# Mixture-of-experts layer: the sum of the experts' rows into the tokens in steps of eight products instead of four

## Chip, cores and metric

One core of a Trainium2 chip runs the whole layer as one program. The time is the device time of one execution in microseconds (us). Three runs of the kernel before gave 1341.96, 1343.40 and 1344.57 us: the median is 1343.4. A trace of one more execution gives what each engine did: TensorE (PE, its weight loads apart as PEld), VectorE (DVE), ScalarE (ACT), GpSimd (POOL) and SyncE (SP), which issues the weight DMAs.

## What is computed

A decoder layer for 512 tokens of width 1024: a mixer (a convolution group and a dilated-attention group), a LayerNorm, a mixture of 32 experts of which each token takes 4, and a second LayerNorm. The change lies in the part with the experts:

```
logits = xt @ router_w + router_b
top_logit, top_idx = top_k(logits, 4);  gate = softmax(top_logit)
# per expert e, for the tokens that chose it:
g = min(xb @ w_gate[e] + b_gate[e], 7);  u = clip(xb @ w_up[e] + b_up[e], -7, 7)
y = ((u + 1) * g * sigmoid(1.702 * g)) @ w_down[e] + b_down[e]
out[token] += gate * y                    # the sum of the change
x = layer_norm(alpha * x + out)
```

All of it is in float32. Each expert has three 1024x1024 matrices, 12 MB, which are read from memory once: some 400 MB in all.

## The kernel before

The mixer and the first LayerNorm take the first 270 us and are the same in both kernels. Behind them comes the main pass over the experts.

**Rows and groups.** A *row* is a set of 32 token slots of one expert. The table `TURNS` gives the order of the experts and how many rows each has: expert 0 has three, then 2, 2, 3, 3, 2, 3, 4, 2, 2, 3, 2, 4, 2, 2, 3, 2, 4, 2, 4, 2, 2, 3, 4, 2, 2, 3, 4, 3, 2, 1, 1 for experts 1 to 31. Here "expert n" is the place in this order. Four rows in a line make a *group* of 128 slots (22 groups). The tokens of a group are gathered with indirect DMAs on POOL, one for each row (L1017). Rows of one expert may lie in one group or in two.

**One expert** (`expert`, L1066) goes through six pieces of weights of 2 MB. Pieces 0 to 3 are gate and up: for each row 8 matmuls into the row's own PSUM bank (L1078; an f32 matmul stands in the trace as two records, so 16 records for a row and piece). After piece 3, each row goes through `swiglu` on DVE and ACT (L1059 to L1064), which ends with the transposed hidden values `hT`. Pieces 4 and 5 are the down product: two rows of one group together (L1104, 512 columns) or one row (L1107, 256 columns). It can start when `hT` of its rows is there. At the end ACT and DVE write the result as an upper part `yh` and a lower part `yl` (L1121, L1123).

**The sum** (`combine`, L1125) adds a group's rows to the 512 tokens in `acc`: a one-hot matrix `cg` from DVE (L1129), then for each of four tiles of 128 tokens and each half of the columns two products, `cg` with `yh` and `cg` with `yl`, into one PSUM bank of the pool `cb` (L1135, L1136), and one add on DVE (L1137). That is 16 products and 8 adds for a group. The pool `cb` has three banks; `gd` has four for the experts' own results and `sl` has one.

**What sets the order.** Each engine takes its instructions in the order in which they are written. `combine` is a generator: it stops at each `yield`, and `fill` goes on with it up to the next one. After each of an expert's six pieces `tick` calls `fill` once (`FILLS` is six ones), so that one step stands behind each piece. What stands between piece 3 and piece 4 stands on PE between the last gate and up product and the first down product, which waits for `hT`. A group's sum is put in line (L1494 in the kernel before) when the next expert uses no row of it any more. Before the last expert's end `ENDC` lets all that is left run in one go.

Of the kernel before, what the change touches and what calls it, by code (L numbers as in the profile page):

```python
# [27 lines left out]
# Experts are taken in an order of falling token count (expert 0 first, whatever its count); the  # L28
# place in that order sets how many blocks of 32 token slots an expert gets in the main pass.
# Tokens beyond an expert's slots are taken by the loop behind it, 128 at a time.  # L30
# [3 lines left out]
# the blocks of the places, in the order of the main pass: light and heavy ones take turns, as the loads set the pace  # L34
# [3 lines left out]
def plan():  # L38
    """Places in the order that the main pass takes them, each with its rows (group, row)."""
    by = {n: [p for p in range(1, NE) if NBLK[p] == n] for n in (4, 3, 2, 1)}  # L40
    seq = [0] + [by[int(n)].pop(0) for n in TURNS[1:]]
    rows, n = [], 0
    for p in seq:
        if p == seq[-1]:
            n = -(-n // 4) * 4
        rows.append((p, [((n + b) // 4, (n + b) % 4) for b in range(NBLK[p])]))
        n = max(n + NBLK[p], 4)
    return rows, -(-n // 4)


# column ranges of the constant array
# [28 lines left out]
# how many working buffers the mixer has  # L80
# [10 lines left out]
# how many of a channel's taps the tensor engine makes, and GpSimd adds up  # L91
# [23 lines left out]
class Buf:  # L115
    """Space of one kind: taken when the first task that uses it is placed, given back after the last."""
# [5 lines left out]
class Plan:  # L122
    """The order of a long stretch of instructions: tasks with an engine, a rough duration (us) and what they
    read and write are placed one by one where they can start first; of several, the one with the longest
    path behind it (less its group's lag) goes first. Spaces of a kind are given out in program order; of a bank,
    one engine has to be done before another can begin."""
# [58 lines left out]
    def order(self, lags):  # L185
        """[(start, end, task, engine, {space: place})]"""
# [78 lines left out]
def tile_layer(ctx: ExitStack, tc: tile.TileContext, x, positions, w_in, conv_w, conv_b, conv_ln_g,  # L265
# [22 lines left out]
    def piece():  # L288
        """The next place of the ring, when there is room."""
        i = turn.pop(0)  # L290
        turn.append(i)
        count[0] += 1
        return ring[i].rearrange("p (k a) f -> p k (a f)", a=2)

    def expert_loads(tag, e):
        """The six loads of one expert's weights."""
# [22 lines left out]
    def advance(used=1):  # L319
        """Pieces have been used up: start the loads that now have room."""  # L320
        freed[0] += used
        while stream and count[0] - freed[0] < size[0]:
            stream.pop(0)()
# [24 lines left out]
    # ================= mixer =================  # L348
# [24 lines left out]
    def warm(t, n):  # L373
        """Products that nobody reads: the tensor engine's clock is halved after a pause."""
        for _ in range(n):
            P.matmul(t.rearrange("p (a c) -> p a c", a=4), onesb, onesb[:, None, :].to_broadcast([128, 4, 128]), start=True,
                     stop=True)

    class Late:
        """Space that another use has had before."""  # L380
# [9 lines left out]
    # Working space in pieces, for the projections and the attention, then taken anew for the second half. Between the  # L390
    # transposes of x and the residual, x's place holds more keys, queries and values.
# [20 lines left out]
    def copy(n, dst, src, r, w, **kw):  # L412
        """A copy that either of two engines can make."""
        def f(e):
            (S.activation(dst(), src(), AF.Copy) if e == "A" else V.tensor_copy(dst(), src()))  # L415
        return op("AV", (0.05 + n / 1180, 0.07 + n / 960), f, r, w, **kw)

# [103 lines left out]
    last_pass, conv_last, RING = [], {}, dict(gt=0, a=1, k=2, q=3, v=0)  # L521

    def unit(n, c, pairs=False):
        """x @ w for 128 channels, in three float32r passes; two heads' first halves come before their second ones."""
# [28 lines left out]
    def conv(c):  # L553
        """The first taps as products with diagonal matrices, the next summed by GpSimd, the others added to the products."""
# [46 lines left out]
    def sbuf_tt(o, a, b, opr, r, w, **kw):  # L601
        """An operation on two arrays in SBUF, which either of two engines can make."""
# [8 lines left out]
    # the out projection's operands in upper and lower parts  # L611
# [15 lines left out]
    def pair(c):  # L627
        """q, k, v and the attention of one pair of heads."""
# [23 lines left out]
        def head(tt, h):  # L652
# [6 lines left out]
            # s = -(score / 8 + mask), its least value  # L659
# [37 lines left out]
    pws = []  # L697

    def conv_tail():
        pl.group = "tail"  # L700
        def total(v, key):
            """u[:, 0] = v(0) + .. + v(3), then its sum over partitions."""
# [121 lines left out]
    def bias_parts(gu):  # L824
        pl.group = "bias"
        """Gate or up biases in three bf16 parts, (part, expert) on partitions."""
# [54 lines left out]
    for tt in range(TT):  # L881
# [12 lines left out]
        def choose(e, lst=lst, lg=lg, tt=tt):  # L894
            """The four experts of each token."""
# [32 lines left out]
    # expert 0 comes first whatever the counts: its ranks need no order  # L928
# [11 lines left out]
    # what it takes from here to the first gather  # L940
# [3 lines left out]
    # expert 0's gate and up weights  # L944
# [25 lines left out]
    # ================= experts =================  # L970
# [11 lines left out]
    def hot(members, rank):  # L982
        """One-hot of tokens by slot. Members: (place, first row, rows, first block)."""
# [10 lines left out]
    def by_slot(members, oh, auxp, ps, cols):  # L994
        """Columns of aux by slot."""
# [6 lines left out]
    def by_row(used, ss, ps, cols):  # L1002
        """Columns of ss, each row of slots on all four quarters of the partitions."""
# [4 lines left out]
    def gather(st, sv):  # L1008
        """The rows of x1 that the slots name."""
# [21 lines left out]
    def slots(members, rank, auxp, pool=(sl, "sl")):  # L1031
        """One-hot of tokens by slot; then each slot's token and gate, and the gather of the tokens' rows."""
# [33 lines left out]
    def expert(tag, rows, sel, tick, pool=(gd, "gd"), small=lambda: None, keep=False):  # L1066
        """rows: (group state, row). Gate and up, SwiGLU, down; tick() runs between the pieces."""
# [57 lines left out]
    def combine(st):  # L1125
        """acc += one-hot^T y, in steps."""
# [4 lines left out]
        for tt in range(TT):  # L1131
# [6 lines left out]
            yield  # L1138
# [24 lines left out]
    def last_load():  # L1163
        """A place of the ring, held to the end: down biases, the second LayerNorm's scale and shift."""
# [9 lines left out]
    def begin(i):  # L1174
        """The first half of the slots of the groups that place i of the order newly takes."""
# [26 lines left out]
    # the first group, expert 0 alone: its tokens, then the order of the experts, at last its gates  # L1202
# [22 lines left out]
    # counts and the order of the experts  # L1225
# [21 lines left out]
    # (behind the first gather, so that the next weights come after it)  # L1247
# [3 lines left out]
    # the gates: softmax over each token's four, spread over the experts, in three bf16 parts  # L1251
# [22 lines left out]
    def setup():  # L1274
        """Everything permuted into the order of the experts; the next groups."""
# [31 lines left out]
    def add_bias():  # L1307
        """acc += sum over experts of gate * b_down; then the second LayerNorm's vectors on all partitions."""
# [31 lines left out]
    def overflow():  # L1340
        """Tokens past each place's slots: how many rounds of 128, and where each place's rounds start."""
# [7 lines left out]
        # inclusive running sum over places  # L1349
# [8 lines left out]
    def rounds():  # L1358
        """The tokens past the slots."""
# [44 lines left out]
    # ================= second LayerNorm =================  # L1404
    def stats(z):
        """Mean and deviation of rows of z."""
# [7 lines left out]
    def outputs():  # L1414
        """The output without the last expert's sum; then acc's rows of its slots."""
# [29 lines left out]
    def quarter(t, q):  # L1445
        """The columns of quarter q, for the partitions that hold it."""
        return t[q * 32:(q + 1) * 32].rearrange("p (b q c) -> p q b c", b=8, q=4)[:, q]

    def last_rows():
        """The rows of the last expert's tokens, a quarter of the columns in each quarter of the partitions."""  # L1450
# [16 lines left out]
    done = 0  # L1467
    first = setup()
    new = []
    for i, (p, rows) in enumerate(order):  # L1470
        def tick(c):
            """Work for other groups, between an expert's pieces."""
# [24 lines left out]
    # the last expert: between its pieces come all other sums and the output that they make; then the tokens past  # L1497
    # the slots, if any; at last its own tokens' rows are made anew
# [6 lines left out]
    # an empty slot's row lies outside  # L1505
# [8 lines left out]
    def tick(c):  # L1514
# [8 lines left out]
        if c == 4:  # L1523
            # (the square root's table, before it is waited for)
# [35 lines left out]
```

## Time and profile before

| what | value |
|---|---|
| device time, median of three | 1343.4 us (1341.96 to 1344.57) |
| span of the profiled execution | 1349.2 us |
| PE busy | 1279.9 us, 95% |
| DVE busy | 680.5 us, 50% |
| ACT busy | 293.8 us, 22% |
| POOL busy | 190.6 us, 14% |
| memory read | 436.64 MB |

The profiled execution has a time of its own: its span is 5.8 us above the median of the runs. The main pass lies between 270 and 1320 us of it. The trace counts an engine as busy from an instruction's start to its modelled end; matmuls on different quarters of the array overlap, so that their mean duration is some five times their distance. A row of a timeline merges equal instructions that follow each other: start, length, engine, line, what is written and read, how many, and in brackets how long the engine was idle before and what ended that. In the trace PE's clock has two levels: 1.00 is 2.4 GHz, 0.50 is 1.2 GHz.

### The profile page before, as it was taken

How to read it: one execution, taken by the hardware profiler on the slowest of the kernel's cores; microseconds unless marked ns; L12 is line 12 of the kernel's file. 1: busy time of each engine (PE TensorE's matmuls, PEld its weight loads, DVE VectorE, ACT ScalarE, POOL GpSimd, SP SyncE). 2: the span in 40 equal slices, each digit the busy share in tenths (PEclk: the TensorE clock that was granted, in tenths of full speed). 3: DMA queues.
4: the chain of work that ended last, by engine and by line, in shares of the span. 5: the costliest groups of instructions: out<-in, count | busy, mean ns of one | idle time of the engine just before them, and what ended most of it. 6: DMA issues, size and time to landing. Idle time of an engine off the chain costs nothing. (4 is left out here: it accounts for less than half of the span.)

```text
span 1349.2 us, 27298 instructions
## 1 busy us (share of the span) xinstructions
PE 1279.9 (95%) x11407; PEld 578.0 (43%) x11407; DVE 680.5 (50%) x1605; ACT 293.8 (22%) x588; POOL 190.6 (14%) x163
## 2 busy tenths in 40 slices
PE   8989999799999999999999999999999999999993
PEld 7767757533243344433333233435433333433241
DVE  6999764754343443544354343534443543354364
ACT  5677774211011010111010011111110100111022
POOL 2863110511101110101001101010201020000002
PEclk9999999799999999999999999999999999999996
DMA  9400334799999998999999999999999999978991
GB/s 293 145 1 25 105 128 127 291 338 380 406 409 406 406 405 318 379 408 405 405 387 397 405 406 407 386 389 352 403 407 408 349 396 407 371 274 334 397 403 70
DMA packets 126250, 442.72 MB, mean 328 GB/s; under 512 B 8359, under 2 KB 16695, under 8 KB 126124
## 3 DMA queue, kind: packets, MB, share of 16 engines
q1 hardware_dynamic: 122092, 429.98, 82.6%
q0 software_dynamic: 4032, 10.95, 2.4%
q8 instruction: 92, 1.51, 0.5%
q14 instruction: 34, 0.28, 0.1%
HBM read 436.64 MB, written 4.33 MB: 327 GB/s over the span
## 5 line engine op out<-in xcount | busy, mean ns | idle before, releaser
L1078 PE MATMUL gd<-wt,xTg 128*32 128x512 f32 x4592 | 522.7, 593 | 1.4 <-DVE xTg L1053 1.4
L1078 PEld LDWEIGHTS gd<-wt,xTg 128*32 128x32 f32 x4592 | 151.4, 110 | 300.6 <-issue 286.5
L1017 POOL DMA_INDIRECT xg<-x1d,idx x83 | 79.6, 959 | 913.4 <-DVE tk L1046 871.2
L1137 DVE TENSOR_TENSOR acc<-acc,cb 128x512 f32<-128x512 f32 x168 | 107.1, 678 | 181.1 <-PE cb L1136 180.9
L1104 PE MATMUL gd<-wt,hT 128*32 128x512 f32 x1344 | 172.4, 605 | 15.4 <-DVE hT L1064 11.1
L1060 ACT ACTIVATE sg<-gm 128x256 f32<-128x256 f32 x83 | 34.6, 417 | 624.7 <-DVE gm L1059 590.1
L1123 DVE TENSOR_TENSOR yl<-gd,wh 32x256 fp32r<-32x256 f32 (+1 forms) x172 | 86.3, 502 | 131.9 <-ACT wh L1121 130.1
L1121 ACT ACTIVATE wh<-gd 32x256 fp32r<-32x256 f32 (+1 forms) x172 | 75.8, 441 | 274.2 <-PE gd L1104 164.1
L1107 PE MATMUL gd<-wt,hT 128*32 128x256 f32 x1600 | 100.3, 380 | 2.9 <-issue 1.3
L1104 PEld LDWEIGHTS gd<-wt,hT 128*32 128x32 f32 x1344 | 50.1, 111 | 115.1 <-issue 85.9
L1059 DVE TENSOR_SCALAR gm<-gd 128x256 f32<-128x256 f32 x82 | 32.8, 400 | 118.3 <-PE gd L1078 118.3
L546 PE MATMUL bk<-wt,wh 128*128 128x512 f32 (+1 forms) x352 | 80.8, 377 | 1.5 <-ACT wh L415 0.8
L1135 PE MATMUL cb<-wh,cg 128*128 128x512 f32 (+1 forms) x168 | 75.4, 449 | 2.0 <-DVE cg L1129 2.0
L1107 PEld LDWEIGHTS gd<-wt,hT 128*32 128x32 f32 x1600 | 57.9, 110 | 44.4 <-issue 12.1
L1078 PE MATMUL gd<-wb,xTg 128*32 128x512 f32 x656 | 76.6, 593 | 0.0
L546 PEld LDWEIGHTS bk<-wt,wh 128*128 128x128 f32 x352 | 61.0, 189 | 14.6 <-ACT wh L415 1.3
L584 DVE SCALAR_TENSOR_TENSOR bk<-u,cT,bk 128x512 f32<-128x512 f32 x88 | 66.2, 752 | 1.8
L1136 PE MATMUL cb<-yl,cg 128*128 128x512 f32 (+1 forms) x168 | 66.8, 398 | 0.0
L1135 PEld LDWEIGHTS cb<-wh,cg 128*128 128x128 f32 (+1 forms) x168 | 32.0, 190 | 56.6 <-issue 36.3
L1063 DVE SCALAR_TENSOR_TENSOR um<-um,tk,sg 128x256 f32<-128x256 f32 x83 | 42.1, 508 | 9.5
L546 PE MATMUL bk<-wt,wl 128*128 128x512 f32 (+1 forms) x176 | 41.8, 379 | 2.3 <-DVE wl L537 2.1
L1011 DVE TENSOR_REDUCE tk<-sl 128x4 f32<-128x8 f32 (+2 forms) x21 | 3.5, 166 | 77.3 <-PE sl L1005 77.3
(336 smaller groups left out, 1259.9 us busy)
## 6 DMA issues: line engine op xcount, KB each, us to landing
wt<-in_exp_w_gate_dram SPq DMA_DIRECT2D x112, 1024.0 KB
wt<-in_exp_w_up_dram SPq DMA_DIRECT2D x112, 1024.0 KB
wt<-in_exp_w_down_dram SPq DMA_DIRECT2D x52, 2048.0 KB
wb<-in_exp_w_down_dram SPq DMA_DIRECT2D x12, 2048.0 KB
wb<-in_exp_w_gate_dram SPq DMA_DIRECT2D x16, 1024.0 KB
wb<-in_exp_w_up_dram SPq DMA_DIRECT2D x16, 1024.0 KB
wt<-in_w_in_dram SPq DMA_DIRECT2D x3, 2048.0 KB
acc<-in_x_dram SPq DMA_DIRECT2D x8, 512.0 KB
```

The costliest lines, as they stand in the source:

```text
L546: P.matmul(b.t[:, ts], w.t[:, k], xx[:, k, ts], start=(pas == 0 and k == 0), stop=(pas == 2 and k == KT - 1))
L584: op("V", 0.663, (lambda j: lambda e: V.scalar_tensor_tensor(b.t, u[:, c, j:j + T], cT[:, c, j:j + 1], b.t, op0=OP.mult, op1=OP.add))(j), ...
L1017: G.indirect_dma_start(out=xg[:, r], out_offset=None, in_=x1d[:, :], in_offset=bass.IndirectOffsetOnAxis(ap=idx[:, r:r + 1], axis=0))
L1063: V.scalar_tensor_tensor(um, um, st["tk"][:, 8 + r:9 + r], sg, op0=OP.mult, op1=OP.mult)
L1078: P.matmul(ps[i][q * 32:(q + 1) * 32], st["xT"][:, r, c * 2 + k], w[:, k, :, :, q], start=False, stop=(c == 3 and k == 1))
L1104: P.matmul(d[j * 32:(j + 1) * 32], st["hT"][:, r + j % 2, c * 4 + k], w[:, k, 2 * (j // 2):2 * (j // 2) + 2], **kw)
L1107: P.matmul(d[j * 32:(j + 1) * 32, 0:256], st["hT"][:, r, c * 4 + k], w[:, k, j], **kw)
L1121: S.activation(st["yh"][o], a, AF.Copy)
L1123: V.tensor_tensor(st["yl"][o], a, st["yh"][o].bitcast(F32), OP.subtract)
L1135: P.matmul(ps, cg[0:n, tt * 128:(tt + 1) * 128], st["yh"][0:n, c], start=True, stop=False)
L1136: P.matmul(ps, cg[0:n, tt * 128:(tt + 1) * 128], st["yl"][0:n, c], start=False, stop=True)
L1137: V.tensor_tensor(acc[:, tt, c], acc[:, tt, c], ps, OP.add)
```

## The change

The `yield` at the end of a tile of 128 tokens is now made after the second and the fourth tile only. The other lines of the diff remove comments and doc strings, which make no instruction, and shift the line numbers behind the change by one.

```diff
     def combine(st):
...
         yield
         for tt in range(TT):
             for hf in range(2):
                 c = slice(hf * 512, (hf + 1) * 512)
                 ps = cb.tile([128, 512], F32, name="cb")
                 P.matmul(ps, cg[0:n, tt * 128:(tt + 1) * 128], st["yh"][0:n, c], start=True, stop=False)
                 P.matmul(ps, cg[0:n, tt * 128:(tt + 1) * 128], st["yl"][0:n, c], start=False, stop=True)
                 V.tensor_tensor(acc[:, tt, c], acc[:, tt, c], ps, OP.add)
-            yield
+            if tt % 2:
+                yield
```

The number of instructions stays the same on every engine, and ACT, POOL and SP keep their order. On PE and DVE the products and adds move. PE in expert 5, from piece 2 on, before (`wt_1922` and `wt_1979` are pieces 2 and 3 of its gate and up weights, `wb_1986` is its first piece of down weights):

```order
L1078 MATMUL gd<-wt_1922,xTg 32x512 x16
L1135 MATMUL cb<-wh,cg 128x512
L1136 MATMUL cb<-yl,cg 128x512
L1135 MATMUL cb<-wh,cg 128x512
L1136 MATMUL cb<-yl,cg 128x512
L1078 MATMUL gd<-wt_1979,xTg 32x512 x16
L1135 MATMUL cb<-wh,cg 128x512
L1136 MATMUL cb<-yl,cg 128x512
L1135 MATMUL cb<-wh,cg 128x512
L1136 MATMUL cb<-yl,cg 128x512
L1104 MATMUL gd<-wb_1986,hT 32x512 x16
```

The same place of PE after the change:

```order
L1078 MATMUL gd<-wt_1922,xTg 32x512 x16
L1135 MATMUL cb<-wh,cg 128x512
L1136 MATMUL cb<-yl,cg 128x512
L1135 MATMUL cb<-wh,cg 128x512
L1136 MATMUL cb<-yl,cg 128x512
L1135 MATMUL cb<-wh,cg 128x512
L1136 MATMUL cb<-yl,cg 128x512
L1135 MATMUL cb<-wh,cg 128x512
L1136 MATMUL cb<-yl,cg 128x512
L1078 MATMUL gd<-wt_1979,xTg 32x512 x16
L1104 MATMUL gd<-wb_1986,hT 32x512 x16
```

Four products have gone from behind piece 3 to behind piece 2, and nothing stands between the last gate and up product and the down product any more. The four that stood behind piece 4 have moved ahead as well, so that pieces 1 and 2 are followed by eight each.

DVE at the end of the same expert, before (two rows, then the adds of the step behind piece 3, the transposition for the next group, the adds of the step behind piece 4, and the lower parts):

```order
L1064 STREAM_TRANSPOSE hT<-um 128x256
L1137 TENSOR_TENSOR acc<-acc,cb 128x512 x2
L1053 STREAM_TRANSPOSE xTg<-xg 128x1024
L1137 TENSOR_TENSOR acc<-acc,cb 128x512 x2
L1123 TENSOR_TENSOR yl<-gd,wh 64x512 x2
```

DVE from the four small operations of piece 1 on, after the change, in the same expert:

```order
L1046 TENSOR_REDUCE tk<-sl 128x4
L1137 TENSOR_TENSOR acc<-acc,cb 128x512 x8
L1059 TENSOR_SCALAR gm<-gd 128x256
L1061 TENSOR_SCALAR um<-gd 128x256
L1062 SCALAR_TENSOR_TENSOR um<-um,gm 128x256
```

All eight adds stand ahead of `swiglu` now, and none behind it.

## Rows read from the trace of the kernel before

**Rows 1.** The page: busy us of each engine, share of the span, instructions.
```profile
PE 1279.9 (95%) x11407; PEld 578.0 (43%) x11407; DVE 680.5 (50%) x1605; ACT 293.8 (22%) x588; POOL 190.6 (14%) x163
```

**Rows 2.** Main pass as one window: busy us of PE, PEld, DVE, ACT, POOL; clock, DMA.
```profile
300.00:1300.00 1000.00, 981.02 (x9694) 369.16 (x9686) 430.44 (x1086) 112.91 (x257) 72.06 (x76) 1.00 0.99 387
```

**Rows 3.** Waits of PE and PEld, 300 to 1300 us: total, times, longest.
```profile
PE gd L1104 <- DVE hT L1064: 11.2, 12, 1.1
...
PEld gd L1104 <- DVE hT L1064: 24.1, 16, 2.0
...
PEld gd L1104 <- DMA wt<-in_exp_w_up_dram: 0.7, 2, 0.4
```

**Rows 4.** Timeline of PE, expert 9 (two rows): steps behind pieces 1, 2 and 3.
```profile
577.12 0.50 PE L1135 MATMUL cb<-wh,cg 128*128 128x512 f32 x1
577.46 0.40 PE L1136 MATMUL cb<-yl,cg 128*128 128x512 f32 x1
...
577.93 0.40 PE L1136 MATMUL cb<-yl,cg 128*128 128x512 f32 x1
...
581.83 0.50 PE L1135 MATMUL cb<-wh,cg 128*128 128x512 f32 x1
...
586.51 0.50 PE L1135 MATMUL cb<-wh,cg 128*128 128x512 f32 x1
```

**Rows 5.** Timeline of PE, expert 7 (four rows, no step): pieces 0 to 3, then down.
```profile
506.83 22.50 PE L1078 MATMUL gd<-wt,xTg 128*32 128x512 f32 x208
529.14 1.91 PE L1107 MATMUL gd<-wt,hT 128*32 128x256 f32 x32
```

**Rows 6.** Timelines of PE: expert 6 (three rows, step), 10 (three, none), 16 (two, none).
```profile
487.97 0.51 PE L1135 MATMUL cb<-wh,cg 128*128 128x512 f32 x1
...
489.10 3.74 PE L1104 MATMUL gd<-wt,hT 128*32 128x512 f32 x32
...
621.15 3.21 PE L1104 MATMUL gd<-wt,hT 128*32 128x512 f32 x27 [0.77 <-DVE hT L1064]
...
815.37 5.39 PE L1107 MATMUL gd<-wt,hT 128*32 128x256 f32 x96 [0.20 <-DVE hT L1064]
```

**Rows 7.** Timeline of all engines, expert 5 (two rows of one group, with steps).
```profile
443.01 0.26 PE L1005 MATMUL sl<-ss,rows 128*128 128x5 bf16 x4
...
447.97 0.95 POOL L1017 DMA_INDIRECT xg<-x1d,idx  x1 [0.30 <-issue]
...
448.59 0.39 PE L1136 MATMUL cb<-yl,cg 128*128 128x512 f32 x1
...
449.99 1.28 DVE L1137 TENSOR_TENSOR acc<-acc,cb 128x512 f32<-128x512 f32 x2 [4.79 <-PE cb L1136]
451.19 0.42 DVE L1059 TENSOR_SCALAR gm<-gd 128x256 f32<-128x256 f32 x1
...
455.71 0.64 PE L1104 MATMUL gd<-wb,hT 128*32 128x512 f32 x4 [1.06 <-DVE hT L1064]
```

**Rows 8.** Timeline of all engines, expert 14 (two rows of one group, no step).
```profile
741.14 0.25 PE L1005 MATMUL sl<-ss,rows 128*128 128x5 bf16 x4
741.33 7.07 PE L1078 MATMUL gd<-wt,xTg 128*32 128x512 f32 x64
...
746.10 0.95 POOL L1017 DMA_INDIRECT xg<-x1d,idx  x1 [0.31 <-issue]
748.19 0.42 DVE L1059 TENSOR_SCALAR gm<-gd 128x256 f32<-128x256 f32 x1 [6.04 <-PE gd L1078]
...
750.58 1.02 PE L1104 MATMUL gd<-wt,hT 128*32 128x512 f32 x2 [2.18 <-issue]
...
752.72 4.79 PE L1104 MATMUL gd<-wt,hT 128*32 128x512 f32 x28 [1.11 <-DVE hT L1064]
```

**Rows 9.** Two windows of two us in expert 14, columns as in rows 2.
```profile
752.00:754.00 2.00, 1.28 (x8) 0.40 (x12) 1.97 (x6) 0.00 (x0) 0.00 (x0) 0.64 1.02 408
754.00:756.00 2.00, 2.00 (x12) 0.39 (x8) 1.58 (x11) 0.00 (x0) 0.00 (x0) 0.51 1.04 414
```

## The prediction

> **What bounds the kernel now.** First the page, for the engines' busy shares, then a table of windows over the main pass, then the waits of PE, and last timelines of single experts. On the page PE is busy for 95% of the span [rows 1], and in the main pass for 981 of 1000 us, while the DMA engines are busy for 99% of it and the weights come at 387 GB/s [rows 2]. Two resources that are both full look alike in these views; the waits tell them apart. PE's largest named wait is for `hT`, 11.2 us by its matmuls and 24.1 us by its weight loads, and the largest for a DMA is 0.7 us [rows 3]. So the weights are there when PE wants them, PE's own queue sets the time, and what a change puts on PE between two gate and up pieces is paid in full. What it puts where PE waits for `hT` anyway is free. DVE has 430 of 1000 us to do [rows 2] and matters only where PE waits for it.
>
> **What the change does, part by part.** The generator can be followed on paper. For 20 of the 22 groups `fill` makes the one-hot matrix behind piece 0 of one expert, and before the change the four steps stand behind its pieces 1, 2, 3 and 4. Now two steps of eight products stand behind pieces 1 and 2, and nothing behind 3 and 4. The experts are 1, 3, 5, 6, 8, 9, 11, 12, 13, 15, 17, 18, 20, 21, 23, 24, 25, 27, 28 and, one piece later, 30. Expert 0's group 0 is among these sums, group 20 is summed in one go in both kernels, and the last group in another way.
>
> *A step of four.* Piece 2 of expert 9 with the step before it takes 581.83 - 577.12 = 4.71 us, piece 3 with its step 586.51 - 581.83 = 4.68 [rows 4]. The 32 records of such a piece alone take 3.43, at 22.31/208 = 0.107 us a record in expert 7 [rows 5]. A step therefore costs 1.25 us. Two products more cost 577.93 - 577.46 = 0.47 [rows 4], so that four products are 0.94 and the change over and back 0.31. A step of eight is 1.25 + 0.94 = 2.19.
>
> *Moved ahead.* Behind pieces 1 and 2: 2 x 0.94 = 1.88 us more. Behind piece 4, where PE does not wait: 1.25 less. That is +0.63 for an expert, less x, what the step behind piece 3 really cost.
>
> *The step behind piece 3.* With three rows x is 0: in expert 6 the step runs from 487.97 to 489.10 and the down product follows without a wait, while in expert 10, without a step, PE comes early and waits, 0.77 us of it named [rows 6]. With four rows no pause is left even without a step (gate and up to 529.14, down at 529.14 [rows 5]), so x is 1.25 for the two of the four such experts (17, 27) whose first down unit is one row. For 12 and 23 it is a pair of rows, which no row shows without a step: x lies between 0 and 1.25, and I take 0.7. With two rows the step is covered too, but the adds of the step behind piece 2 delay `swiglu`: its first operation stands at 451.19, at the end of the adds, where the first row's products were done by 450.9 (piece 3 from 448.9, 1.72 for 16 records, 0.3 to the result) [rows 7]. Hence x = 0.3 for the ten two-row experts that have a gather, and 0 for expert 9, which has none; expert 16 shows how little is waited for between the rows when nothing is in the way, 0.20 us [rows 6].
>
> Sum: three rows 4 x 0.63 = 2.5; expert 9 0.6; two rows 10 x 0.33 = 3.3; four rows 2 x (0.63 - 1.25) + 2 x (0.63 - 0.7) = -1.4; expert 30 about 0, between -1 and +1. Together **+5.0 us**.
>
> *Banks.* A step of eight fills four banks, and `cb` has three, so the fourth pair of products waits for the first add. With a prompt DVE this just fits: the first pair is done 0.34 + 0.40 = 0.74 us after the step's start [rows 4], an add takes 0.64 [rows 7], which makes 1.4, and the fourth pair's turn comes at 0.58 + 2 x 0.47 = 1.5. It does not fit where the products' release comes late. In expert 5 the second pair behind piece 2 ended at 448.98 and the first 0.47 before, and DVE, idle for 4.79 us, began to add at 449.99 only. In expert 14 the first row of piece 3 ended near 748.40 - 1.72 = 746.7, and DVE began at 748.19 although it had been idle for 6.04 us. Both are 7.0 us after the `L1005` of the new group (443.01, 741.14) and 2.0 us after its fourth gather began on POOL (447.97, 746.10) [rows 7, 8]. Why, the trace does not say; I take it as bound to the gather. After the change the step behind piece 2 begins 0.1 + 2.19 + 3.43 = 5.7 us after `L1005`, its first pair ends at 6.5, is released at 7.0, and its bank is free at 7.65, where the fourth pair wants it at 7.2: 0.45 us of wait in each of ten experts, **+4.5 us**. If the release were prompt it would be nothing; at the lateness of expert 5, 1.5 us each, it would be 15.
>
> *The clock.* In the six experts with two rows of one group (1, 5, 11, 13, 24, 25; expert 1 has a few small products of the overflow count there) both rows' `hT` are needed at once. `swiglu` takes 455.71 - 451.19 = 4.5 us for both [rows 7] and can begin 1.7 us before the last gate and up product ends, a row's 16 records, so that without a step PE pauses for 2.8 us but for two records. With the step, which ended at 448.9 + 3.43 + 1.25 = 453.6, the pause was 455.71 - 453.6 = 2.1. In expert 14 it was 4.3 (748.4 to 752.72) [rows 8], and behind it the clock stood at 0.64 and then 0.51, that is mostly 1.2 instead of 2.4 GHz, for four us [rows 9]: 0.36 x 2 + 0.49 x 2 = 1.7 us lost. 2.8 lies between the pause that kept the clock and the one that lost it; I let half of the six lose it, 3 x 1.7 = **+5.1 us**, between 0 and 10.
>
> *The sum.* 5.0 + 4.5 + 5.1 = 14.6 us. It comes from one execution with a span of 1349.2, 5.8 us above the median of the runs; as a difference of waits and steps it applies to the median as well: 1343.4 + 14.6 = **1358.0 us**. The DMAs give nothing back: their issues keep their place behind the pieces, and a slower PE only leaves the ring of weights fuller.
>
> **The rivals.** *The long pause.* The release stays late where it now falls on the first row of piece 3, as in expert 14, and all six pauses grow to 4.3 us and lose the clock. For it: 14 is the only shape of this kind without a step that the rows show. Against it: the longer steps put that row's end some 10.6 us after `L1005`, well behind the 7.0. It would add 6 x (4.3 - 2.8) + 3 x 1.7 = 14.1 us: 1372.
>
> *Every pause loses the clock.* The pauses are the 2.8 us of the forecast, and all six are followed by a stretch at 1.2 GHz: 3 x 1.7 = 5.1 us more, 1363. For it: expert 14 lost the clock though two records ran in its pause. Against it: the clock's mean over the main pass is 1.00 [rows 2], so that the covered pauses of 2.1 us cannot have lost it often, and 2.8 is nearer to 2.1 than to 4.3. [...]
>
> *Faster.* There are 40 steps fewer, and each carries 0.31 us of changing over. If PE no longer waits after piece 3, since DVE has fewer adds in its way there, x is 1.25 everywhere and each expert gains 0.62: 20 x 0.62 = 12.4 us, 1331. It decides where x passes 0.63. For it: the four-row experts, where it is so. Against it: expert 10 waits without any add in the way [rows 6].
>
> *The loads set the pace.* 99% of DMA and 387 GB/s [rows 2] speak for it, 0.7 us of waits for DMAs [rows 3] against it. Then PE's losses are hidden, and the time stays at 1343.
>
> **How the numbers follow.** About 2.7 us, 0.2%, is what a measurement of this kernel can tell from no change. Slower by the steps and waits above, with the unknown costs anywhere between their middle and their lower ends (1346 to 1362): 0.52, of which the lower quarter has neither bank waits nor clock losses (1348). Every pause loses the clock: 0.15. The long pause: 0.20. No change: 0.06. Faster: 0.07. That makes 0.87 for slower. The range of 8 in 10 goes from 1347 to 1372: it leaves out faster and no change, 0.13, and some 0.07 above, where late banks (up to 10 us more) and the long pause meet.
>
> **What would show it.** In the profile after: PE's waits for `hT` in front of L1104 should grow from 11.2 to some 25 us, and waits of PE for the adds of L1137 should appear, about 4 us, in the two-row experts with a gather. Experts 17 and 27 should be shorter by about 0.6 us, three-row experts longer by 0.6. The clock should show some new stretches at half, behind experts 5, 11, 13, 24 or 25 alone. The adds behind piece 2 should begin about 7.0 us after `L1005`, and `swiglu` right after the first row of piece 3. The forecast is wrong if the waits for `hT` do not grow, if the adds hold the fourth pair for over a microsecond, or if PE comes to wait for weights.

## The result and the profile after

The changed kernel takes 1358.2 us (1357.34 to 1359.73), the kernel before 1343.8: ratio 1.0108 [1.0094, 1.0122], 14.4 us slower. The forecast was 1358.0.

The experiments fell on three chips, which are of two kinds. On chip 1 (e1 to e4) the kernel before takes 1344.0 us, as above; on chip 0 (e5 to e8) and chip 10 (e9, e10) it takes 1352.1 and 1351.9, some 8 us more. On chip 0 the changed kernel takes 1366.5, ratio 1.0113 [1.0098, 1.0128], again 14.4 us slower. Below, "faster chip" and "slower chip" stand for the two kinds. The trace ahead of the prediction, with its span of 1349.2, is like those of the slower chips, and is compared here with the changed kernel's second profile (e8_after, span 1363.8). On the faster chip the kernel before has a span of 1340.6 (e1_before) and the changed one 1355.5. The two differences of spans are 14.6 and 14.9.

The changed kernel on the faster chip: busy us of each engine, then the main pass as one window (columns as in [rows 1, 2]).

```profile
PE 1281.6 (95%) x11407; PEld 606.1 (45%) x11407; DVE 679.6 (50%) x1605; ACT 293.7 (22%) x588; POOL 190.4 (14%) x163
...
300.00:1300.00 1000.00, 973.10 (x9622) 391.52 (x9614) 427.08 (x1082) 109.83 (x252) 71.84 (x76) 1.00 0.99 385
```

The busy shares are those of [rows 1], but for 45% instead of 43% of PEld, with fewer records in the same 1000 us than [rows 2] and a clock that still has the mean 1.00: the same work, more slowly. PE's busy time in the window fell by some 11 us on either kind of chip (from 984.64 in e1 to 973.10, and from 981.02 [rows 2] to 969.69 in e8), since it waits more. Its waits, answering to [rows 3], first on the faster chip (where e1 has 9.6 and 21.8 us for `hT` by PE and PEld), then on the slower:

```profile
PE gd L1104 <- DVE hT L1064: 15.9, 19, 1.1
PE cb L1135 <- DVE acc L1137: 1.4, 1, 1.4
...
PEld gd L1104 <- DVE hT L1064: 34.1, 22, 2.0
PEld cb L1135 <- DVE acc L1137: 14.6, 41, 1.8
```

```profile
PE gd L1104 <- DVE hT L1064: 15.5, 18, 1.1
...
PE cb L1135 <- DVE acc L1137: 2.0, 10, 0.2
```

Two waits are larger: for `hT`, where the step behind piece 3 used to stand, and for the adds, in front of the products of the sum. The second is seen best by the weight loads, which PE makes ahead of a product: 38 of the 41 loads belong to nineteen experts with two steps each and wait 0.31 us on average. The other three are in expert 30, whose steps stand one piece later. Its second step of eight lies behind its piece 3, where the add that frees a bank stands on DVE behind `swiglu`; there the fourth pair itself waits:

```profile
1299.65 0.50 PE L1135 MATMUL cb<-wh,cg 128*128 128x512 f32 x1 [1.40 <-DVE acc L1137]
```

Expert 9 on the faster chip, PE, answering to [rows 4]:

```profile
582.45 3.64 PE L1078 MATMUL gd<-wt,xTg 128*32 128x512 f32 x32
...
586.36 0.40 PE L1136 MATMUL cb<-yl,cg 128*128 128x512 f32 x1
...
586.83 0.40 PE L1136 MATMUL cb<-yl,cg 128*128 128x512 f32 x1
...
587.29 0.39 PE L1136 MATMUL cb<-yl,cg 128*128 128x512 f32 x1
...
587.88 0.39 PE L1136 MATMUL cb<-yl,cg 128*128 128x512 f32 x1
588.20 3.64 PE L1078 MATMUL gd<-wt,xTg 128*32 128x512 f32 x32
592.54 1.72 PE L1107 MATMUL gd<-wt,hT 128*32 128x256 f32 x28 [0.70 <-DVE hT L1064]
```

A piece with its step of eight takes 588.20 - 582.45 = 5.75 us, where a piece with a step of four takes 4.68 [rows 4]: 1.07 more. The second products of the four pairs show where: the third comes 0.46 behind the second (587.29 - 586.83), the fourth 0.59 behind the third. The last row is the pause that was filled before: PE waits for `hT`.

### The profile page after: what moved, and what is told of

Same layout as the page of the kernel before. It is cut to its first block, busy times and chain, and to the rows that moved or that the text cites. A ratio compares the mean times of both kernels' runs of the same rounds, so it can differ in the third digit from the quotient of the medians.

```text
span 1355.5 us, 27299 instructions
## 1 busy us (share of the span) xinstructions
PE 1281.6 (95%) x11407; PEld 606.1 (45%) x11407; DVE 679.6 (50%) x1605; ACT 293.7 (22%) x588; POOL 190.4 (14%) x163
## 5 line engine op out<-in xcount | busy, mean ns | idle before, releaser
L1078 PE MATMUL gd<-wt,xTg 128*32 128x512 f32 x4592 | 535.3, 594 | 2.6 <-DVE xTg L1053 2.6
L1078 PEld LDWEIGHTS gd<-wt,xTg 128*32 128x32 f32 x4592 | 167.5, 110 | 294.5 <-issue 269.6
L1104 PE MATMUL gd<-wt,hT 128*32 128x512 f32 x1344 | 176.5, 594 | 17.2 <-DVE hT L1064 12.9
L1137 DVE TENSOR_TENSOR acc<-acc,cb 128x512 f32<-128x512 f32 x168 | 104.3, 682 | 121.4 <-PE cb L1136 121.3
L1107 PE MATMUL gd<-wt,hT 128*32 128x256 f32 x1600 | 105.6, 380 | 5.7 <-PE gd L1078 3.0
L1104 PEld LDWEIGHTS gd<-wt,hT 128*32 128x32 f32 x1344 | 54.4, 110 | 119.2 <-issue 76.5
L1107 PEld LDWEIGHTS gd<-wt,hT 128*32 128x32 f32 x1600 | 60.7, 110 | 49.1 <-issue 8.4
L546 PEld LDWEIGHTS bk<-wt,wh 128*128 128x128 f32 x352 | 61.5, 190 | 14.4 <-ACT sg L590 1.4
L1075 PE MATMUL gd<-wl,selr 96*32 96x512 bf16 x316 | 52.3, 381 | 0.0
L1104 PE MATMUL gd<-wb,hT 128*32 128x512 f32 x320 | 43.0, 617 | 2.9 <-DVE hT L1064 2.9
```

The source lines that it names most:

```text
L546: P.matmul(b.t[:, ts], w.t[:, k], xx[:, k, ts], start=(pas == 0 and k == 0), stop=(pas == 2 and k == KT - 1))
L1075: P.matmul(ps[i][q * 32:(q + 1) * 32], sel[0:96], bv[:, :, :, q], start=True, stop=False)
L1078: P.matmul(ps[i][q * 32:(q + 1) * 32], st["xT"][:, r, c * 2 + k], w[:, k, :, :, q], start=False, stop=(c == 3 and k == 1))
L1104: P.matmul(d[j * 32:(j + 1) * 32], st["hT"][:, r + j % 2, c * 4 + k], w[:, k, 2 * (j // 2):2 * (j // 2) + 2], **kw)
L1107: P.matmul(d[j * 32:(j + 1) * 32, 0:256], st["hT"][:, r, c * 4 + k], w[:, k, j], **kw)
L1137: V.tensor_tensor(acc[:, tt, c], acc[:, tt, c], ps, OP.add)
```

## The experiments

**e1_before: the kernel before, once more.**

> The kernel before once more, unchanged, for a second profile. Theory A (the profile that the prediction was made from is typical): span near 1349 us in the profile, experts 2 and 14 again 26.8 us long from their first bias product to the next expert's, the clock at half behind expert 14's pause. Theory B (that execution was a long one of its own, since its span is 5.8 us above the median of the runs): span near 1342, experts 2 and 14 near 24.6 us as in the changed kernel, and the same experts 8, 9, 13, 18, 20, 21 and 24 as in the first profile within 0.2 us. Timed against itself the ratio is 1.000 within 0.002 in either.

Measured: 1342.3 us against 1344.0, ratio 0.9995 [0.9982, 1.0007], span 1340.6. Experts 2 and 14 took 23.7 us each, less than the 24.6 of theory B, and experts 8, 13, 18, 20, 21 and 24 were 0.25 to 0.29 shorter than in the first profile, where theory B had them within 0.2. In the main it is theory B all the same: the long pause of expert 14 [rows 8] and the half clock behind it [rows 9] are not in this trace. Expert 5 and expert 14 in it, PE, DVE and POOL:

```profile
440.11 0.26 PE L1005 MATMUL sl<-ss,rows 128*128 128x5 bf16 x4
...
445.23 0.40 PE L1136 MATMUL cb<-yl,cg 128*128 128x512 f32 x1
...
445.66 1.28 DVE L1137 TENSOR_TENSOR acc<-acc,cb 128x512 f32<-128x512 f32 x2 [3.37 <-PE cb L1136]
448.00 0.42 DVE L1059 TENSOR_SCALAR gm<-gd 128x256 f32<-128x256 f32 x1 [1.05 <-PE gd L1078]
...
737.16 0.26 PE L1005 MATMUL sl<-ss,rows 128*128 128x5 bf16 x4
...
742.10 0.95 POOL L1017 DMA_INDIRECT xg<-x1d,idx  x1 [0.30 <-issue]
...
742.77 0.42 DVE L1059 TENSOR_SCALAR gm<-gd 128x256 f32<-128x256 f32 x1 [4.61 <-PE gd L1078]
```

The adds behind piece 2 begin as soon as their first pair is done (445.23 + 0.40), 5.55 us after `L1005` and not 7.0 as in [rows 7], and `swiglu` in expert 14 begins 5.61 us after it and not 7.05 [rows 8]. So the late release is no property of the kernel. It is there in all seven traces of the slower kind, where in such experts DVE's first operation on PE's results begins 6.9 to 7.1 us after `L1005` (once, in expert 5 of e6, 6.2), and in none of the five of the other, where it begins with the results, from 5.55 us on.

**e2_cover: only the step behind piece 3 is moved.**

```diff
-            yield
+            if tt != 1:
+                yield
+            if tt == 2:
+                yield
```

> Only the step behind piece 3 is moved (to piece 2, which then has eight products); the steps behind pieces 1 and 4 stay. A step of eight costs 5.75 - 3.43 = 2.32 us in the changed kernel's trace and one of four 1.25, so 1.07 more for each expert, less x, the real cost of the step behind piece 3. Theory A (the forecast's: that step stood in a pause and was nearly free, x between 0 and 0.3 but for the four-row experts): 13 us slower, near 1357, plus clock losses of some us. Theory B (no cover: that step was paid in full like the others, x = 1.25): 20 x (1.07 - 1.25) = 4 us faster, near 1340.

Measured: 1360.4 us, ratio 1.0133 [1.0115, 1.0152], 16.4 us slower. Theory A: this one move makes all of the loss and some 2 us more. Expert 6 shows the emptied pause, which answers to the filled one of [rows 6]:

```profile
487.55 1.02 PE L1104 MATMUL gd<-wt,hT 128*32 128x512 f32 x2
488.89 3.21 PE L1104 MATMUL gd<-wt,hT 128*32 128x512 f32 x27 [0.32 <-DVE hT L1064]
```

**e3_484: the cover stays, the step behind piece 4 moves to piece 2.**

```diff
-            yield
+            if tt != 1:
+                yield
```

> The step behind piece 3 stays, the one behind piece 4 moves to piece 2, which then has eight products. Theory A (a step costs what PE spends on it): 20 x (1.07 - 1.25) = 4 us faster, near 1340, less some tenths for each two-row expert whose swiglu is held by four adds instead of two. Theory B (the products of the step behind piece 2 are released late, up to 7 us behind the group's small products, so that the fourth pair waits for a bank for 1 to 1.5 us in ten experts): 10 to 15 us slower than that, 1350 to 1355.

Measured: 1341.3 us, ratio 0.9980 [0.9970, 0.9991], 2.8 us faster. Theory A, near its 4 us. This was on a faster chip, where the adds follow their products at once; for the slower chips it says nothing on theory B.

**e4_646: steps of 6, 4 and 6.**

```diff
                 V.tensor_tensor(acc[:, tt, c], acc[:, tt, c], ps, OP.add)
-            yield
+                if (tt, hf) in ((1, 0), (2, 0), (3, 1)):
+                    yield
```

> Steps of 6, 4 and 6 products behind pieces 1, 2 and 3, none behind 4; no step needs a fourth bank. Theory A (change over of 0.31 us for a step, 0.47 for a pair; the step behind piece 3 is covered in experts of two and three rows, paid in those of four): piece 1 +0.47, piece 3 0 or +0.47, piece 4 -1.25: 16 x 0.78 + 4 x 0.31 = 14 us faster, near 1330. Theory B (the step behind piece 3 is not covered, or its third pair is not): 20 x 0.31 = 6 us faster, near 1338. Theory C (the loads or other waits take what PE saves): no change, 1344.

Measured: 1334.6 us, ratio 0.9939 [0.9925, 0.9954], 9.4 us faster, between theories A and B: the third pair behind piece 3 is covered only in part. In experts with two rows of two groups it takes 8.45 us from the end of the last gate and up product to the next expert, in the changed kernel, with the pause unfilled, 8.08, so the third pair costs 0.37 of its 0.47 there. The profiled run also lost the clock behind the pause of expert 2, which the edit does not touch; that expert took 25.4 us instead of 23.7.

**e5_448: eight products in the pause.**

```diff
-            yield
+            if tt < 2 or tt == 3:
+                yield
```

> Steps of 4, 4 and 8 products behind pieces 1, 2 and 3, none behind 4. The step of eight stands in the pause, but its fourth pair needs a bank that only the first add gives free, and this add stands behind swiglu on DVE. Theory A (the banks bind): in experts of two and three rows PE gets past the fourth pair only about 1.3 us after the last hT is ready (an add of 0.65, a pair of 0.47, the change over), so that with the four products that piece 2 saves against steps of 4, 8 and 4 (-1.07) and the pause (free before, 1.3 too long now) it is 1341 + 20 x (1.3 - 1.07) or more: 1345 to 1365. Theory B (the pause takes them all): 20 x 1.07 = 21 us faster than with 4, 8 and 4, near 1320.

Measured: 1401.2 us, ratio 1.0357 [1.0341, 1.0373], 49 us slower. Theory A in kind, but far above its range. Expert 6, PE and DVE:

```profile
498.83 0.39 PE L1136 MATMUL cb<-yl,cg 128*128 128x512 f32 x1
501.54 0.62 PE L1135 MATMUL cb<-wh,cg 128*128 128x512 f32 x1 [2.33 <-DVE acc L1137]
...
502.52 4.94 PE L1104 MATMUL gd<-wt,hT 128*32 128x512 f32 x32
...
498.29 0.45 DVE L1064 STREAM_TRANSPOSE hT<-um 128x256 f32<-128x256 f32 x1
...
500.84 2.47 DVE L1137 TENSOR_TENSOR acc<-acc,cb 128x512 f32<-128x512 f32 x4
```

The add that frees a bank stands on DVE behind `swiglu` of all three rows, and the down product of the first two rows, for which `hT` was ready at 498.74, waits behind the fourth pair on PE: not 1.3 us but 3.8 (502.52 - 498.74). I had counted from the last `hT`; with three or four rows the first unit could start well before it. Behind this pause the clock fell (0.50 from 502 to 504 us): the fourth pair's products take 0.62 and 0.63 us instead of 0.4, and the down product 4.94 instead of 3.6.

**e6_drop3 and e7_drop4: the price of a step by itself.**

```diff
         for tt in range(TT):
+            if tt == 2:            # 3 in e7_drop4
+                yield
+                continue
             for hf in range(2):
```

> The step behind piece 3 is left out of the kernel before: its four products and two adds (the third tile of 128 tokens) are not computed; the other steps stay where they are. It gives the price of that step by itself. Theory A (it stands in PE's pause; real price 0 in experts of two and three rows, 0.67 in 12 and 23, 1.2 in 17 and 27, 1.25 in 30 where it stands one piece later, 0.94 in the last expert): 6 us faster, near 1338, less 1.7 for each pause that now loses the clock (1338 to 1342). Theory B (paid like the others): 20 x 1.25 + 0.94 = 26 us faster, near 1318.

> The step behind piece 4 is left out of the kernel before: its four products and two adds (the fourth tile of 128 tokens) are not computed. The price of a step where PE does not wait. Theory A (1.25 us each, as piece lengths show): 20 x 1.25 + 0.94 = 26 us faster, near 1318. Theory B (hidden in part by another limit, as the loads): less than 13 us faster.

Measured, against 1352.1 on chip 0: without the step behind piece 3 1346.8 us, ratio 0.9957 [0.9945, 0.9969], 5.3 us faster; without the step behind piece 4 1325.9, ratio 0.9808 [0.9795, 0.9822], 26.2 us faster. The same four products cost 26 us in one place and 5 in the other. Expert 6 without its step in the pause:

```profile
490.99 1.02 PE L1104 MATMUL gd<-wt,hT 128*32 128x512 f32 x2
492.33 3.21 PE L1104 MATMUL gd<-wt,hT 128*32 128x512 f32 x27 [0.32 <-DVE hT L1064]
```

It took 36.96 us from its first bias product to the next expert's, with the step 36.94: the price there is 0. Between the two traces it is within 0.1 us of 0 in every expert of two or three rows but 5, which lost the clock in its emptied pause, 0.70 and 0.68 in experts 12 and 23, 1.15 in 17 and 27, 1.27 in 30.

**e8_after: the changed kernel once more.**

> The changed kernel once more, for a second profile: does each of the six pauses of experts 1, 5, 11, 13, 24 and 25 lose the clock by chance? Theory A (the loss is chance, one of six in the first profile): again none to two of them at half clock, not the same ones, time near 1358. Theory B (bound to the place): expert 5 again alone, and the start of expert 0 again. In either the adds begin 0.04 us behind their products.

Measured: 1366.5 us against 1352.1. Of the six emptied pauses one lost the clock, that of expert 24, where it had been that of expert 5 in the first profile: theory A. The windows of two us behind each, first expert 5 on the faster chip, with expert 11's in the last line for comparison, then expert 24 in e8:

```profile
456.00:458.00 2.00, 1.06 (x8) 0.33 (x12) 1.97 (x4) 0.00 (x0) 0.00 (x0) 0.86 1.04 414
458.00:460.00 2.00, 2.00 (x16) 0.51 (x12) 1.81 (x13) 0.00 (x0) 0.00 (x0) 0.50 1.02 406
460.00:462.00 2.00, 2.00 (x20) 0.56 (x16) 0.00 (x0) 0.00 (x0) 0.00 (x0) 0.79 1.04 408
656.00:658.00 2.00, 2.00 (x20) 0.53 (x19) 0.93 (x1) 0.00 (x0) 0.00 (x0) 1.00 1.03 412
```

```profile
1105.00:1107.00 2.00, 2.00 (x12) 0.39 (x8) 2.00 (x9) 0.00 (x0) 0.00 (x0) 0.50 1.04 412
1107.00:1109.00 2.00, 2.00 (x18) 0.46 (x14) 0.04 (x1) 0.00 (x0) 0.00 (x0) 0.72 1.02 406
```

Expert 5 lost 0.14 x 2 + 0.50 x 2 + 0.21 x 2 = 1.7 us by it. The expectation on the adds (0.04 us behind their products) failed: chip 0 releases the products late again. Expert 5 on it:

```profile
445.09 0.25 PE L1005 MATMUL sl<-ss,rows 128*128 128x5 bf16 x4
...
447.40 3.64 PE L1078 MATMUL gd<-wt,xTg 128*32 128x512 f32 x32
...
451.31 0.39 PE L1136 MATMUL cb<-yl,cg 128*128 128x512 f32 x1
...
452.80 0.50 PE L1135 MATMUL cb<-wh,cg 128*128 128x512 f32 x1 [0.18 <-DVE acc L1137]
...
453.46 2.78 PE L1078 MATMUL gd<-wt,xTg 128*32 128x512 f32 x24
...
450.04 0.95 POOL L1017 DMA_INDIRECT xg<-x1d,idx  x1 [0.30 <-issue]
...
452.06 2.48 DVE L1137 TENSOR_TENSOR acc<-acc,cb 128x512 f32<-128x512 f32 x4 [3.59 <-PE cb L1136]
455.45 0.42 DVE L1059 TENSOR_SCALAR gm<-gd 128x256 f32<-128x256 f32 x1 [0.92 <-PE gd L1078]
```

The first add begins 452.06 - 445.09 = 6.97 us after `L1005` and 2.02 after the fourth gather, the two numbers of [rows 7]. The fourth pair waits, and piece 2 with its step takes 453.46 - 447.40 = 6.06 us instead of 5.75. `swiglu` waits for PE's own products and no longer for adds.

**e9_pauses and e10_646: use the pauses of the experts without a sum.** In e9 `combine` takes a list of steps in pairs of products; a group whose next expert has no sum and two or three rows is spread over both.

```diff
+            free = i + 2 < NE and order[i + 2][1][0][0] == order[i + 1][1][0][0] and len(order[i + 2][1]) < 4
+            combs.append(combine(GS[done], (2, 0, 3, 0, 0, 0, 0, 0, 3) if free else (3, 2, 3)))
-            combs.append(combine(GS[done]))
```

> Steps of 6, 4 and 6 products as in e4, but seven groups whose next expert has two or three rows and no sum of its own (experts 1, 3, 9, 13, 15, 21, 25) take 4 behind piece 1, 6 behind piece 3 and the last 6 behind piece 3 of that next expert. Theory A (what stands in a pause is free or costs 0.37 us, what stands elsewhere costs 1.25 and 0.47 for each pair over two): against e4 each of the seven saves 0.47 + 1.25, less 0 in experts 2 and 14 and 0.37 in 4, 10, 16, 22 and 26: 10 us, ratio to the kernel before 0.986. Theory B (the pauses of experts without a sum are no cover, or the adds that now stand behind swiglu there hold what follows): no gain over e4, ratio 0.994 or above.

> The kernel of e4 once more, for a comparison with e9 on the same chip. Theory A and B: ratio to the kernel before 0.994 within 0.002. Theory A of the pauses (pieces behind which PE waits): if this is a chip on which the products' releases come late, the step of four behind piece 2 fits its three banks and no wait of PE for an add appears.

Measured, on chip 10: e9 1331.2 us against 1351.9, ratio 0.9845 [0.9830, 0.9861], 20.7 us faster than the kernel before; e10 1339.6, ratio 0.9912 [0.9889, 0.9934], a little more than e4 gave and just outside the 0.994 within 0.002 that was expected. As expected, no product of e10 waits for an add between 300 and 1300 us. Theory A of e9: 8.4 us faster than e10, where 10 were expected; the runs of e10 spread over 9 us. Expert 14 in e9, PE, and its windows, answering to [rows 8, 9]:

```profile
737.95 0.39 PE L1138 MATMUL cb<-yl,cg 128*128 128x512 f32 x1
738.93 1.02 PE L1104 MATMUL gd<-wt,hT 128*32 128x512 f32 x2 [0.59 <-PE cb L1138]
741.07 3.21 PE L1104 MATMUL gd<-wt,hT 128*32 128x512 f32 x28 [1.12 <-DVE hT L1064]
```

```profile
740.00:742.00 2.00, 0.94 (x12) 0.34 (x16) 1.92 (x4) 0.00 (x0) 0.00 (x0) 1.00 1.03 412
742.00:744.00 2.00, 2.00 (x24) 0.60 (x20) 2.00 (x5) 0.00 (x0) 0.00 (x0) 1.00 1.02 408
```

The six products stand in the pause, and the clock stays at 1.00 where it fell to 0.64 and 0.51 before. That the products keep it there is not shown: in e10, on the same chip, the pause of expert 14 is as empty as in [rows 8], and behind it the clock stays at 1.00 as well:

```profile
745.54 1.02 PE L1104 MATMUL gd<-wt,hT 128*32 128x512 f32 x2 [2.18 <-issue]
...
748.00:750.00 2.00, 2.00 (x24) 0.65 (x20) 2.00 (x10) 0.00 (x0) 0.00 (x0) 1.00 1.02 406
```

Of the versions that compute the whole layer, e9 gains most on the kernel before.

## Why the prediction was right

The forecast was +14.6 us, the times say +14.4 on either kind of chip. Term by term, with what was measured on a slower chip (from the trace ahead of the prediction to e8) and on a faster one (from e1 to the first profile after):

| term | forecast | slower chip | faster chip |
|---|---|---|---|
| steps behind 1 and 2 grow | 20 x 1.88 = 37.6 | 42.9 | 42.9 |
| step behind 4 gone | -25.0 | -25.3 | -25.3 |
| step behind 3 gone (x) | -7.6 | -7.6 | -4.9 |
| banks, late release | 4.5 | 3.5 | 0 |
| clock behind pauses | 5.1 | 1.7 | 1.7 |
| all ahead of expert 1, not touched by the change | - | 1.0 | 0.9 |
| sum | 14.6 | 16.2 | 15.3 |

The differences of the spans are 14.6 and 14.9. On the slower chip the sum is 1.6 too high; some 1.0 of that, by an estimate from the lengths of the experts, was given back by experts 2 and 14 and by the end behind the main pass, which the change does not touch.

*The bound and the cover.* PE's queue sets the time, and what stands behind piece 3 is covered in experts of two and three rows and paid in those of four: e7 and e6 show it as 26.2 against 5.3 us. The second line is e7's 26.2 (by its interval 24 to 28) less 0.94 for the last expert, where the products were left out too; it is taken for both columns. The third counts 4.9 from e6 by expert (0.70 + 0.68 + 2 x 1.15 + 1.27); for the slower chip the delay of `swiglu` by the adds is added, 0.27 us in each of the ten experts for which I had put 0.3. On the faster chip the adds are done before `swiglu` can start (1.05 us of idle time ahead of it in e1), and that part is 0. The forecast's x of 0 for three rows, 0.7 for experts 12 and 23 and 1.25 for 17 and 27 all came out within 0.1 us.

*Moved ahead: mis-sized.* The step that failed is "a step of eight is 1.25 + 0.94 = 2.19". It is 2.32: 5.75 - 3.43. I had let the fourth pair fit "just" behind a prompt add, 1.4 against 1.5 us. It does not, since the load of its weights too waits for the add: 0.13 us for each of 39 steps, 5 us in all. That it is the fourth pair, for which none of the three banks is left, other lengths bear out: from a step's first product to the next gate and up product four products take 1.12 us, six 1.56 (e4) and eight 2.17 (e3), so that a third pair costs 0.44 and a fourth 0.61. No run gave `cb` a fourth bank. The first line is 19 x 2.14, and 1.04 + 1.19 for expert 30, whose second step holds PE up by the 1.4 us shown above; with what it saves behind pieces 4 and 5, expert 30 as a whole came out 0.27 us shorter, within the forecast's "between -1 and +1".

*Banks: right on one kind of chip.* The rule of 7.0 us after `L1005` held in e8, and its price came out at 0.35 us instead of 0.45. On the faster chip there was no late release, and no price. The forecast took this term from a trace of a slower chip and added it to a median of a faster one; "it applies to the median as well" was wrong for it. That the rule is bound to the gather is not shown: the fourth gather begins 5 us after `L1005` on both kinds (742.10 - 737.16 in e1).

*The clock: mis-sized.* I let three of six pauses lose it, and one did in each profile, a different one each time. A loss has the size that was forecast, 1.7 us. The Trainium skill (TensorE: Matmul & The Clock Gate, HAM oscillation — how this bites in real kernels) tells of a kernel whose array fell back to half its clock at every wait between its bursts, with waits longer than these pauses. It does not say that all six would lose it, and in either trace one of six did. The same six pauses stand empty in e2, where none lost the clock, and in e6, where that of expert 5 did. The longer pause of expert 14 lost it in five of the six slower-chip traces that have it empty, and not in e10. What decides which, these runs do not show. The line on what lies ahead of expert 1 holds on the faster chip a start of expert 0 at half clock, 2.0 us, and a main pass that began 1.2 us earlier; that stretch at half clock came and went among the kernels of this study.

*The signs named.* The waits for `hT` in front of L1104 grew from 11.2 to 15.5, not to 25; in the weight loads from 24.1 to 34. With those in front of L1107 and those put down to something else, all waits of PE in front of a down product grew from 18.2 to 28.2. The waits for adds were there in ten experts, 2.0 us and not 4. One sign of being wrong, adds that hold the fourth pair for over a microsecond, was met in one place, expert 30 (1.4 us), where the second step of eight stands in front of the down product. Experts 17 and 27 became 0.37 us shorter, not 0.6, and three-row experts with the one behind them 0.83 to 0.99 longer, not 0.6: both are the 0.26 by which two steps of eight are dearer. The end of the first row of piece 3, put at 10.6 us after `L1005` against the long pause, comes to 10.4 by the prediction's own numbers, and `swiglu` began there in e8 (455.45 - 445.09).

*The rivals.* "Every pause loses the clock" and "the long pause" are out: one pause in six lost it, and none of the six is 4.3 us long. "The loads set the pace" is out: e7 gave back all 26 us. "Faster" failed by its own condition, x above 0.63: x is near 0 in 14 of 20 experts. Its other half is true: a step saved is 0.31 us saved, where the products are not taken out of the pause. e3 is faster for that, less the dearer fourth pair; e4 and e9 also put more products into pauses.

The sum was closer than its terms, and that is luck. Two errors, +5.3 us of the step of eight and -3.4 of the clock, for the most part took each other out. On the faster chip, where the result was measured, the 4.5 us of the banks were missing too, and 2.7 less of x and 0.9 ahead of expert 1 made up for most of that. The mechanism is not luck: that a step which was free in the pause is paid for in its new place, e2, e6 and e7 show.

## What to carry to other kernels

Work on a saturated engine has a price by place, not by size: four products cost 1.25 us where the engine is busy and nothing where it waits for another engine's result. Look for such pauses first and fill them up to the buffers at hand, but not beyond: one product that needs a buffer freed by work behind the pause blocks all that follows. A group as long as the number of buffers plus one paid for the last one each time here: 0.13 us with a prompt add, 0.48 where the products' release came late.

## What the hardware showed unexpectedly

The two kinds of chip differ in more than time. On chips 0 and 10, which are 8 us slower, and in the trace ahead of the prediction, DVE gets the results of products that PE ended between 5.5 and 7 us after a group's `L1005` only about 7.0 us after it; on the faster chip at once. The cause stays open. What a single trace shows twice, as in [rows 7, 8], can still be the chip's.

A pause can shift the array's quarters against each other, as the order of the records suggests; no run tests it. With `hT` of one row of a pair ready, the two records of the first product run on their quarter, and this quarter stays ahead to the next expert. Expert 2 on the faster chip, in the changed kernel, then in the kernel before:

```profile
338.06 0.38 PE L1075 MATMUL gd<-wl,selr 96*32 96x512 bf16 x1
338.28 0.59 PE L1078 MATMUL gd<-wt,xTg 128*32 128x512 f32 x1
338.47 0.60 PE L1104 MATMUL gd<-wt,hT 128*32 128x512 f32 x3
...
346.42 0.26 PE L1005 MATMUL sl<-ss,rows 128*128 128x5 bf16 x4
```

```profile
337.45 0.40 PE L1075 MATMUL gd<-wl,selr 96*32 96x512 bf16 x4
...
344.99 0.25 PE L1005 MATMUL sl<-ss,rows 128*128 128x5 bf16 x4
```

The new expert's first product stands ahead of three products of the old one, and `L1005` comes 8.36 us behind it instead of 7.54. The expert before looks 0.8 us shorter by it, and this one 0.8 longer, with nothing gained or lost by that. So lengths of single experts are compared together with the next one's.
